# Which pair of gated tiles each place of the down projection takes

## The chip, the cores and the metric

The kernel runs on one core of a Trainium2 chip. The metric is the device time of one execution in microseconds (us); the median of several runs is compared. One profiled execution gives the rows that are quoted. The engines are TensorE (PE, with its weight loads as PEld), VectorE (DVE), ScalarE (ACT), GpSimd (POOL) and SyncE (SP, which here only issues transfers). Each engine works through its own list of instructions in order and waits for the others by semaphores.

## The reference, cut to what matters

The program is one decoder layer over 256 tokens of width 2048 in fp32: a norm, an input projection, attention and pooling heads, an output projection, and then the gated MLP, in which the change lies:

```python
def conv_ffn(h, w_up, conv_w, conv_b, w_down):
    u = h @ w_up                                   # 2048 -> 2 * 5632
    ...                                            # causal convolution of width 3 over the tokens
    gate, val = jnp.split(y, 2, axis=-1)
    return (jax.nn.silu(gate) * val) @ w_down      # 5632 -> 2048
```

The sum over the 5632 gated features may be taken in any order.

## The kernel before

**Splitting.** Each fp32 operand is split into a high part (ACT copies it to `wh`, line 126) and a low part (DVE subtracts, `wl`, line 131), and each product is three matmuls: high by high, low by high and high by low. The weights come in halves of 128 x 1024, one half to a step of the program. The last loop of `layer` runs over these steps: at step u it issues PE's matmuls of step u, the high part of step u+6 and the low part of step u+5, and then what hangs on the step. So the splitting runs five to six steps ahead of PE, on the same ACT and DVE lists that also hold the elementwise work.

**Thirds.** The MLP runs in three thirds of 8, 8 and 6 pairs of gated tiles (a pair is 256 of the 5632 features). For each pair there are two blocks of four steps: the gate block and the value block, each of which accumulates into one PSUM tile of the tag `acc`, which has two buffers. Behind a block, `conv` empties the tile (ACT copies one half, line 451, DVE adds the other, line 452, both written `fs`), multiplies by the norm's factor and runs the convolution. Behind a value block, `value` multiplies by the gate (line 700) and splits the result into `hid` (lines 701 and 702).

**Token sums.** In some places of the down projection a quad (256 features by 1024 outputs by 256 tokens, two by two blocks in each operand) takes seven products of blocks in place of eight, a scheme of Strassen's kind. It needs four sums of blocks of the gated pair. `token_sums` makes them directly behind the pair's `value`: four operations in a row on POOL (line 715), and then the split of the four sums into `sx` by ACT (line 716) and DVE (line 717). ACT's instruction waits for POOL, and the weight splits of the next steps stand behind it on ACT's and DVE's lists.

**Down projection.** When all pairs of a third are made, `down_pair` runs twice, once for each half of the 2048 outputs, over nq places (nq is the number of pairs in the third). Place j takes pair j. `MIXED` says which places go by seven products: 0 and 3 in the first pass and 0, 3, 5 and 6 in the second for eight places; 0, and then 0, 2 and 3, for six. `SUMMED` is their union, {8: [0, 3, 5, 6], 6: [0, 2, 3]}, and before the change it is also the list of pairs for which `token_sums` runs. The first place of a third is one of seven products. Its first half writes into PSUM tiles of other tags, its second half into `ps_down`, two tiles of the tag `acc`: the second of them is the buffer in which the third's last value block was accumulated, and its first matmul (the last of the three groups of three at line 722) must wait until DVE's `fs` (line 452) has emptied it.

Of the kernel before, what the change touches and what calls it, by code (L numbers as in the profile page):

```python
# [57 lines left out]
MIXED = {8: ((0, 3), (0, 3, 5, 6)), 6: ((0,), (0, 2, 3))}  # L58
SECOND = {8: (3, 6), 6: (2,)}
SUMMED = {n: sorted(set(a + b)) for n, (a, b) in MIXED.items()}  # L60


def bucket(n):
# [9 lines left out]
def layer(ctx: ExitStack, tc: tile.TileContext, xT, xtok, wts, par, rel_d, ident_d, icnt_d, out):  # L73
    nc = tc.nc
# [24 lines left out]
    raws, wparts, shift, late = {}, {}, {}, {}  # L99
# [147 lines left out]
    ps = small("ps_start")  # L247
# [253 lines left out]
    steps, hooks = [], []  # L501
# [42 lines left out]
    def after(u, f):  # L544

        hooks.append((u, f))
# [148 lines left out]
    def value(ps, g, j):  # L695
        if j == 0:
            late["hid"] = keep.tile([P, KT, 2, S], F32R, name="hid", tag="c")
        y = conv(ps, NF + 2 * g, 1)
        hid, ks = late["hid"], slice(2 * j, 2 * j + 2)
        nc.vector.tensor_tensor(y, y, late["gate"], op=OP.mult)  # L700
        nc.scalar.activation(hid[:, ks, 0, :], y, AF.Copy)  # L701
        nc.vector.tensor_tensor(hid[:, ks, 1, :], y, hid[:, ks, 0, :].bitcast(F32), op=OP.subtract)
        if j in late["mixed"]:
            token_sums(y, late["mixed"].index(j))

    def token_sums(y, i):

# [16 lines left out]
    def down_pair(bp, nq, final):  # L724


        box, runs, mixed = {}, [], MIXED[nq][bp]
        s_end = 2 * mixed[-1] + 1
        rest = 2 * nq - 1 - s_end

        def hid(k, t):
            return [late["hid"][:, k, a, t * P:(t + 1) * P] for a in range(2)]

        def sums(i, n):
            return [late["sx"][:, i, n, a, :] for a in range(2)]

        def bank(t, b):
            return box["tok"][t][:, b, :]

        def part(w, c):  # L740
            return [p[:, 512 * c:512 * (c + 1)] for p in w]

        def quad_sums(u, j, h):
            if j == 0 and h == 0:
                box["aux"], box["p5"], box["p7"] = aux("ps_p"), small("ps_p5"), small("ps_p7")
                box["tok"] = [acc("ps_down") for t in range(NT)]
            first, last, i = j == 0, j == mixed[-1], SUMMED[nq].index(j)
            if h == 0:
                t13, (s1, s4) = wparts.pop(u + 1), late["s"][seven[u]]
                triple(box["aux"][:, 0, :], hid(2 * j, 0), s1, first, last)  # L750
                triple(box["p5"], sums(i, 0), part(t13, 0), first, last)
                triple(box["p7"], sums(i, 2), part(t13, 1), first, last)
                triple(box["aux"][:, 1, :], sums(i, 1), part(s4, 0), first, last)
            else:
                b2, s4 = wparts.pop(u - 1), late["s"][seven[u - 1]][1]
                triple(bank(0, 1), sums(i, 3), part(b2, 0), first, False, end)
                triple(bank(0, 0), hid(2 * j + 1, 0), part(b2, 1), first, False, end)
                triple(bank(1, 0), hid(2 * j + 1, 1), part(s4, 1), first, False, end)

        def quad(u, j, h):  # L760
            w = wparts.pop(u)
            closes = j == nq - 1 and h == 1
            for n, (a, i) in enumerate(((0, 0), (1, 0), (0, 1))):
                for t in range(NT):
                    for b in range(2):
                        nc.tensor.matmul(bank(t, b), hid(2 * j + h, t)[a], part(w, b if h == 0 else 1 - b)[i],  # L766
                                         start=(t == b == 1 and j == 1 and h == 0 and n == 0), stop=(closes and n == 2),
                                         skip_group_check=end)

        def add_out(t, b, c, src):  # L770
            cols_ = slice((2 * bp + b) * 512 + c.start, (2 * bp + b) * 512 + c.stop)
            x2 = late["x2"][:, t, cols_]
            nc.vector.tensor_tensor(x2, src, x2, op=OP.add)
            return lambda: nc.sync.dma_start(out[:, t, cols_], x2)

        def last_quad(us, j):
            ws = [wparts.pop(u) for u in us]
            full = slice(0, 512)
            add_out(1, 1, full, bank(1, 1))
            ends = [small("ps_end")[:, :256] for _ in range(2)]  # L780
            pieces = [(t, b, full, bank(t, b), False) for t, b in ((0, 0), (0, 1), (1, 0))]
            pieces += [(1, 1, slice(256 * i, 256 * i + 256), ends[i], True) for i in range(2)]
            for t, b, c, ps, first in pieces:
                for h, w in enumerate(ws):
                    w = [p[:, c] for p in part(w, b if h == 0 else 1 - b)]
                    for n, (a, i) in enumerate(((0, 0), (1, 0), (0, 1))):
                        nc.tensor.matmul(ps, hid(2 * j + h, t)[a], w[i], start=(first and h == 0 and n == 0),
                                         stop=(h == 1 and n == 2), skip_group_check=True)
                if t or b:
                    stores = [add_out(t, i, c, bank(t, i)) for i in range(2)] if t == 0 else [add_out(t, b, c, ps)]  # L790
                    for store in stores:
                        store()

        def add_part(n):
            x2 = late["x2"][:, :, 1024 * bp:1024 * (bp + 1)]
            pa_, p7 = box["aux"], box["p7"]
            if n in (0, 2):
                s = late["pool"].tile([P, 4, P], F32, name="s", tag="s").rearrange("p a n -> p (a n)")
                nc.scalar.activation(s, p7 if n else pa_[:, 0, :], AF.Copy)
                nc.vector.tensor_tensor(pa_[:, 1, :], pa_[:, 1, :], s, op=OP.add)  # L800
            elif n == 1:
                nc.vector.tensor_tensor(x2[:, 0, :], pa_.rearrange("p a n -> p (a n)"), x2[:, 0, :], op=OP.add)
            elif n == 3:
                x = x2[:, 1, :].rearrange("p (b n) -> p b n", n=512)
                nc.vector.tensor_tensor(x, pa_[:, 1:2, :].to_broadcast([P, 2, 512]), x, op=OP.add)
            else:
                x = x2[:, :, 512:]
                nc.vector.tensor_tensor(x, box["p5"][:, None, :].to_broadcast([P, 2, 512]), x, op=OP.add)

        def close(u):  # L810
            x2 = late["x2"][:, :, 1024 * bp:1024 * (bp + 1)]
            for t in range(NT):
                nc.vector.tensor_tensor(x2[:, t, :], box["tok"][t].rearrange("p b n -> p (b n)"), x2[:, t, :],
                                        op=OP.add)
                if final:
                    nc.sync.dma_start(out[:, t, 1024 * bp:1024 * (bp + 1)], x2[:, t, :])

        end = final and bp == 1
        for j in range(nq):
            for h in range(2):  # L820
                at = 2 * j + h

                def run(u, j=j, h=h, at=at):
                    if j in mixed:
                        quad_sums(u, j, h)
                    elif end and j == nq - 1:
                        if h == 1:
                            last_quad((u - 1, u), j)
                    else:
                        quad(u, j, h)  # L830
                run.seven = int(bp == 1 and j in SECOND[nq]) if j in mixed and h == 0 else None
                acts = [run]
                for n in range(5):
                    if at == s_end + 1 + n * (rest - 1) // 5:
                        acts.append(lambda n=n: add_part(n))
                if at == 2 * nq - 1 and not end:
                    acts.append(lambda: close(0))
                    run.closes = True
                runs.append(acts)
        return runs  # L840

    for n, (g0, g1) in enumerate(THIRDS):
        after(len(steps), lambda nq=g1 - g0: late.__setitem__("mixed", SUMMED[nq]))
        for g in range(g0, g1):
            steps += feat_block(lambda: late["h"], lambda ps, g=g: gate(ps, g), aux if n and g == g0 else acc)
            steps += feat_block(lambda: late["h"], lambda ps, g=g, j=g - g0: value(ps, g, j))
# [7 lines left out]
    n = len(steps)  # L854
# [29 lines left out]
def chunks(w_in, pool_w, w_out, w_up, w_down):  # L884
# [19 lines left out]
    for g0, g1 in THIRDS:  # L904
        for g in range(g0, g1):
            out += feat(w_up, 256 * g) + feat(w_up, DFF + 256 * g)
        for c0 in range(0, D, 1024):
            for k in range(2 * g0, 2 * g1, 2):
                top, low = (w_down[i * P:(i + 1) * P, c0:c0 + 1024] for i in (k, k + 1))
                out += [top, np.concatenate([low[:, 512:], low[:, :512]], axis=1)]  # L910
    return np.stack([np.concatenate(out[i:i + 2], axis=1) for i in range(0, len(out), 2)])
# [37 lines left out]
```

## Time and profile before

| | |
|---|---|
| median of three runs (lowest, highest) | 1022.37 us (1021.85, 1022.79) |
| profiled execution: its time, its span | 1023.08 us, 1021.3 us |
| mean clock granted to PE | 0.998 |
| PE busy | 1012.7 us, 99% of the span |
| DVE busy | 793.6 us, 78% |
| ACT busy | 554.3 us, 54% |
| POOL busy | 74.7 us, 7% |
| token sums in the program | 11: 44 operations on POOL, 11 on ACT, 11 on DVE |

A row of the trace's list in order of time reads: start in us, duration in us, engine, line, operation, what it writes `<-` what it reads, its shape, how many like it follow one another, and in brackets how long the engine stood idle before it and what ended that. Matmuls overlap: a row's duration is longer than its distance to the next row, so distances between starts are used. The table by stretches gives busy time and, under PEclk, the share of PE's full clock that was granted in the stretch.

### The profile page before, as it was taken

What the parts mean: (1) busy time and instruction counts of PE and PEld (TensorE: products, weight loads), DVE (VectorE), ACT (ScalarE), POOL (GpSimd) and SP (SyncE); (2) the same over time, 40 slices, a digit from 0 to 9 for tenths busy, and PEclk for the clock granted to TensorE, in tenths of its full rate; (3) what the DMA queues carried; (4) which work ended last, traced back from release to release, by engine and by line L of the source; (5) the groups of instructions that cost most, each with busy time, mean ns of one, the idle gap of its engine ahead of it and who ended that gap; (6) DMA issues with size and microseconds to landing.
All of it is one profiled execution on the core that took longest, in us unless ns stands there. A gap on an engine that the chain in (4) does not pass through costs nothing.

```text
span 1021.3 us, 13562 instructions
## 1 busy us (share of the span) xinstructions
PE 1012.7 (99%) x5268; PEld 868.8 (85%) x5268; DVE 793.6 (78%) x994; ACT 554.3 (54%) x747; POOL 74.7 (7%) x98
## 2 busy tenths in 40 slices
PE   9999999999999999999999999999999999999998
PEld 8888888888888888887888888888878888888887
DVE  6966667874567877778998687787899887778897
ACT  6844555564545655555545465565564545556642
POOL 0420004600000000010000000000000000010000
PEclk9999999999999999999999999999999999999999
DMA  9774454475453554444655445455365645545461
GB/s 337 268 286 171 170 175 165 166 296 198 165 197 140 202 210 184 181 165 165 247 207 206 165 168 211 176 199 189 135 243 205 241 164 179 199 166 202 184 233 42
DMA packets 30608, 199.19 MB, mean 195 GB/s; under 512 B 3576, under 2 KB 4472, under 8 KB 7760
## 3 DMA queue, kind: packets, MB, share of 16 engines
q1 hardware_dynamic: 29968, 196.89, 52.6%
q0 software_dynamic: 576, 1.44, 0.6%
q8 instruction: 41, 0.67, 0.3%
q14 instruction: 23, 0.19, 0.1%
HBM read 195.83 MB, written 2.49 MB: 194 GB/s over the span
## 4 chain that ended last, share of the span: by engine, by line
PE 91%; DVE 5%; ACT 2%; issue 1%; POOL 0%; ACTq 0%; DVEq 0%; POOLq 0%
PE ps_feat L187 30%; PE ps_tok L174 17%; PE ps_feat L189 15%; PE ps_down L766 15%; PE ps_v L181 4%; PE ps_p L722 4%; PE ps_down L722 3%; DVE wl L131 2%; ACT wh L126 2%; DVE y L686 1%; PE ps_pool L196 1%; DVE y L684 1%; DVE fs L452 1%; PE ps_s L402 1%; POOL s L715 0%
## 5 line engine op out<-in xcount | busy, mean ns | idle before, releaser
L187 PE MATMUL ps_feat<-x2h,wh 128*128 128x512 f32 x1408 | 488.6, 392 | 0.0
L131 DVE TENSOR_TENSOR wl<-raw,wh 128x1024 fp32r<-128x1024 f32 x358 | 434.8, 1252 | 54.9 <-PE ps_tok L174 27.7
L126 ACT ACTIVATE wh<-raw 128x1024 fp32r<-128x1024 f32 x358 | 360.2, 1050 | 147.2 <-DVE raw L145 69.9
L189 PE MATMUL ps_feat<-x2h,wl 128*128 128x256 f32 x1408 | 393.6, 280 | 0.0
L187 PEld LDWEIGHTS ps_feat<-x2h,wh 128*128 128x128 f32 x1408 | 264.3, 188 | 58.3
L189 PEld LDWEIGHTS ps_feat<-x2h,wl 128*128 128x128 f32 x1408 | 264.3, 188 | 0.1
L766 PE MATMUL ps_down<-wh,hid 128*128 128x512 f32 x432 | 108.3, 393 | 0.0
L766 PEld LDWEIGHTS ps_down<-wh,hid 128*128 128x128 f32 x432 | 82.1, 190 | 17.2
L683 ACT ACTIVATE y<-u,pv 128x256 f32<-128x256 f32 x88 | 48.2, 594 | 74.1 <-DVE u L678 74.1
L174 PE MATMUL ps_tok<-wh,xh 128*128 128x512 f32 x256 | 70.1, 396 | 0.0
L174 PE MATMUL ps_tok<-wh,cat 128*128 128x512 f32 x256 | 68.8, 390 | 0.0
L684 DVE SCALAR_TENSOR_TENSOR y<-u,pv,y 128x256 f32<-128x256 f32 x88 | 42.4, 482 | 29.6 <-ACT y L683 29.6
L715 POOL TENSOR_TENSOR s<-y 128x128 f32<-128x128 f32 x22 | 14.2, 647 | 685.9 <-DVE y L700 429.5
L766 PE MATMUL ps_down<-wl,hid 128*128 128x512 f32 x216 | 57.8, 389 | 0.0
L174 PEld LDWEIGHTS ps_tok<-wh,cat 128*128 128x128 f32 x256 | 47.6, 188 | 9.6
L174 PEld LDWEIGHTS ps_tok<-wh,xh 128*128 128x128 f32 x256 | 47.5, 188 | 9.4
L452 DVE TENSOR_TENSOR fs<-ps_feat,fs 128x512 f32<-128x512 f32 x44 | 30.4, 691 | 29.0 <-ACT fs L451 29.0
L766 PEld LDWEIGHTS ps_down<-wl,hid 128*128 128x128 f32 x216 | 40.7, 188 | 8.5
L187 PE MATMUL ps_feat<-xh,wh 128*128 128x512 f32 x128 | 46.2, 402 | 0.0
L686 DVE SCALAR_TENSOR_TENSOR y<-u,pv,y 128x256 f32<-128x256 f32 x88 | 42.7, 485 | 3.1
L451 ACT ACTIVATE fs<-ps_feat 128x512 f32<-128x512 f32 x44 | 26.1, 592 | 32.7 <-PE ps_feat L189 32.4
L701 ACT ACTIVATE hid<-y 128x512 fp32r<-128x512 f32 x22 | 14.0, 634 | 49.0 <-DVE y L700 49.0
(173 smaller groups left out, 1021.0 us busy)
## 6 DMA issues: line engine op xcount, KB each, us to landing
raw<-in_wts SPq DMA_DIRECT2D x177, 1024.0 KB, 5.0
raw<-in_wts SPq DMA_DIRECT2D x4, 512.0 KB, 7.7
x<-in_xtok SPq DMA_DIRECT2D x1, 2048.0 KB, 9.6
raw<-in_wts SPq DMA_DIRECT2D x7, 256.0 KB, 5.9
xboth<-in_xT SPq DMA_DIRECT2D x4, 256.0 KB, 6.8
T<-band POOLq DMA_DIRECT2D x8, 128.0 KB, 5.7
out<-x SPq DMA_DIRECT2D x2, 512.0 KB, 4.4
out<-x SPq DMA_DIRECT2D x3, 256.0 KB, 2.2
```

Of the source, the lines that this page charges most:

```text
L126: nc.scalar.activation(wparts[u][0], raw(u - 1 if u - 1 in seven else u + 1 if u in seven else u), AF.Copy)
L131: nc.vector.tensor_tensor(wl, raw(u - 1 if u - 1 in seven else u + 1 if u in seven else u), wh.bitcast(F32), op=OP.subtract)
L174: nc.tensor.matmul(ps[:, t, :], act[:, k0 + k, a, t * P:(t + 1) * P], w[:, k * 512:(k + 1) * 512], start=(first and k == 0 and n == 0), st ...
L181: nc.tensor.matmul(ps[:, t, :], act[:, k, a, t * P:(t + 1) * P], w[i], start=(first and n == 0), stop=(last and n == 2))
L187: nc.tensor.matmul(ps, wh[:, ws], act[:, k, :, :], start=(first and n == 0), stop=False, skip_group_check=True)
L189: nc.tensor.matmul(ps[:, S:], wl[:, ws], act[:, k, 0, :], start=False, stop=(last and n == len(ks) - 1), skip_group_check=True)
L452: nc.vector.tensor_tensor(dst, ps[:, :, :S], dst, op=OP.add)
L683: nc.scalar.activation(y[:, m, :], u[:, m, 2:], AF.Identity, scale=cw[2], bias=col(C_CB + f))
L684: nc.vector.scalar_tensor_tensor(y[:, m, :], u[:, m, 1:1 + S], cw[1], y[:, m, :], op0=OP.mult, op1=OP.add)
L686: nc.vector.scalar_tensor_tensor(y[:, m, :], u[:, m, :S], cw[0], y[:, m, :], op0=OP.mult, op1=OP.add)
L722: nc.tensor.matmul(ps, act[a], w[i], start=(first and n == 0), stop=(last and n == 2), skip_group_check=skip)
L766: nc.tensor.matmul(bank(t, b), hid(2 * j + h, t)[a], part(w, b if h == 0 else 1 - b)[i], start=(t == b == 1 and j == 1 and h == 0 and n == ...
```

## The change

Place j now takes pair `ORDER[nq][j]`. The places that go by seven products take the pairs that are made first, and the other places take the rest in rising order:

`ORDER = {8: [0, 4, 5, 1, 6, 2, 3, 7], 6: [0, 3, 1, 2, 4, 5]}`

So `token_sums` runs behind pairs 0, 1, 2, 3 where it ran behind 0, 3, 5, 6 (thirds of eight), and behind 0, 1, 2 where it ran behind 0, 2, 3 (the third of six). The places themselves, with seven or eight products each, stay, and the host lays the rows of `w_down` in the new order, so that the transfers keep their number, size and order.

```diff
+ORDER = {n: [js.index(j) if j in js else len(js) + j - sum(i < j for i in js) for j in range(n)]
+         for n, js in SUMMED.items()}
...
         if j in late["mixed"]:
-            token_sums(y, late["mixed"].index(j))
+            token_sums(y, j)
...
-            first, last, i = j == 0, j == mixed[-1], SUMMED[nq].index(j)
+            first, last, i, k = j == 0, j == mixed[-1], SUMMED[nq].index(j), 2 * ORDER[nq][j]
...
-                triple(box["aux"][:, 0, :], hid(2 * j, 0), s1, first, last)
+                triple(box["aux"][:, 0, :], hid(k, 0), s1, first, last)
...
-                        nc.tensor.matmul(bank(t, b), hid(2 * j + h, t)[a], part(w, b if h == 0 else 1 - b)[i],
+                        nc.tensor.matmul(bank(t, b), hid(2 * ORDER[nq][j] + h, t)[a], part(w, b if h == 0 else 1 - b)[i],
...
-        after(len(steps), lambda nq=g1 - g0: late.__setitem__("mixed", SUMMED[nq]))
+        after(len(steps), lambda nq=g1 - g0: late.__setitem__("mixed", range(len(SUMMED[nq]))))
...
-            for k in range(2 * g0, 2 * g1, 2):
+            for k in (2 * (g0 + g) for g in ORDER[g1 - g0]):
```

PE's and SP's lists and POOL's are the same before and after, by operation, shape, tile name and awaited engine; on ACT and DVE only the split of the sums changes its place. The first place is ACT's list behind the value block of pair 6 of the first third, the last pair but one (rows of `hid` end a pair's `value`; `s512h` is the first weight sum of the down projection, which is split within the steps of the last pair). Before:

```order
L451 ACTIVATE fs<-ps_feat 128x512
L683 ACTIVATE y<-u_1880,pv 128x256 x2
L701 ACTIVATE hid<-y 128x2x256
L716 ACTIVATE sx<-s 128x4x128
L126 ACTIVATE wh<-raw 128x1024 x3
L150 ACTIVATE s512h_1871<-raw 128x512
L126 ACTIVATE wh<-raw 128x1024
```

The same place after the change:

```order
L453 ACTIVATE fs<-ps_feat 128x512
L685 ACTIVATE y<-u_1880,pv 128x256 x2
L703 ACTIVATE hid<-y 128x2x256
L128 ACTIVATE wh<-raw 128x1024 x3
L152 ACTIVATE s512h_1871<-raw 128x512
L128 ACTIVATE wh<-raw 128x1024
```

The row of `sx`, which waits for POOL, is gone from between `hid` and the weight splits (lines are two higher in the changed file). The same holds behind pair 5. The second place is DVE's list behind the value block of pair 1 of the first third. Before:

```order
L700 TENSOR_TENSOR y<-y 128x512
L702 TENSOR_TENSOR hid<-y,hid 128x2x256
L131 TENSOR_TENSOR wl<-raw,wh 128x1024 x4
L452 TENSOR_TENSOR fs<-ps_feat,fs 128x512
L678 TENSOR_TENSOR u_1879<-fs,rrow_2591 128x2x256
```

The same place after the change:

```order
L702 TENSOR_TENSOR y<-y 128x512
L704 TENSOR_TENSOR hid<-y,hid 128x2x256
L719 TENSOR_TENSOR sx<-s,sx 128x4x128
L133 TENSOR_TENSOR wl<-raw,wh 128x1024 x4
L454 TENSOR_TENSOR fs<-ps_feat,fs 128x512
L680 TENSOR_TENSOR u_1879<-fs,rrow_2591 128x2x256
```

The split of the sums now stands behind pair 1, ahead of the four weight splits of the next gate block; ACT's list changes alike there, and both change alike behind pair 2.

More of the change, by code (lines that the diff above doesn't have):

```diff
@@ L756, in quad_sums @@
                 triple(bank(0, 1), sums(i, 3), part(b2, 0), first, False, end)
-                triple(bank(0, 0), hid(2 * j + 1, 0), part(b2, 1), first, False, end)
-                triple(bank(1, 0), hid(2 * j + 1, 1), part(s4, 1), first, False, end)
+                triple(bank(0, 0), hid(k + 1, 0), part(b2, 1), first, False, end)
+                triple(bank(1, 0), hid(k + 1, 1), part(s4, 1), first, False, end)
         def quad(u, j, h):
@@ L786, in last_quad @@
                     for n, (a, i) in enumerate(((0, 0), (1, 0), (0, 1))):
-                        nc.tensor.matmul(ps, hid(2 * j + h, t)[a], w[i], start=(first and h == 0 and n == 0),
+                        nc.tensor.matmul(ps, hid(2 * ORDER[nq][j] + h, t)[a], w[i], start=(first and h == 0 and n == 0),
                                          stop=(h == 1 and n == 2), skip_group_check=True)
```

## The prediction

> **What bounds the kernel now.** The page gives PE 99% of the span, so only a wait of PE can be won. The view of waits for PE has two rows (waited for: us in total, times, longest):
>
> ```profile
> PE ps_down L722 <- DVE fs L452: 4.0, 2, 2.0
> PE ps_start L249 <- DVE ones L246: 1.1, 1, 1.1
> ```
>
> The second is the start. The first is the second half of the first place of a down projection: its last group of matmuls waits for DVE to empty the last value block. There are three thirds but two such waits, so I looked at all three in the order of time: the last matmul before the group, the group, the first matmul of the next place, and, in the first two, the start of the next place of seven products, two ordinary places later.
>
> ```profile
> 475.99 0.39 PE L722 MATMUL ps_down<-wl,hid 128*128 128x512 f32 x1
> 478.38 0.73 PE L722 MATMUL ps_down<-s1024h,hid 128*128 128x512 f32 x2 [2.00 <-DVE fs L452]
> ...
> 479.18 3.57 PE L766 MATMUL ps_down<-wh,hid 128*128 128x512 f32 x8
> ...
> 491.69 0.62 PE L722 MATMUL ps_p<-s512h,hid 128*128 128x512 f32 x2
> ...
> 740.39 0.39 PE L722 MATMUL ps_down<-wl,hid 128*128 128x512 f32 x1
> 742.78 0.73 PE L722 MATMUL ps_down<-s1024h,hid 128*128 128x512 f32 x2 [2.00 <-DVE fs L452]
> ...
> 743.58 1.99 PE L766 MATMUL ps_down<-wh,hid 128*128 128x512 f32 x8
> ...
> 754.47 0.61 PE L722 MATMUL ps_p<-s512h,hid 128*128 128x512 f32 x2
> ...
> 958.80 0.39 PE L722 MATMUL ps_down<-wl,hid 128*128 128x512 f32 x1
> 959.02 0.61 PE L722 MATMUL ps_down<-s1024h,hid 128*128 128x512 f32 x2
> ...
> 959.70 1.98 PE L766 MATMUL ps_down<-wh,hid 128*128 128x512 f32 x8
> ```
>
> The third third passes the same point without a stop: 0.22 us between starts, where the others need 2.39. In the first third the row at 479.18 is also slow (3.57 against 1.99 us for the same eight matmuls). The view by stretches shows why (PE, PEld, DVE, ACT and POOL busy, then PEclk):
>
> ```profile
> 476.00:478.40 2.40, 0.40 (x3) 0.03 (x1) 2.37 (x4) 1.33 (x2) 0.00 (x0) 1.00 1.00 406
> 478.40:480.00 1.60, 1.60 (x5) 1.32 (x6) 0.93 (x2) 0.92 (x2) 0.00 (x0) 0.74 0.98 389
> 480.00:482.00 2.00, 2.00 (x6) 1.59 (x5) 1.89 (x5) 0.17 (x1) 0.00 (x0) 0.50 0.48 197
> 482.00:484.00 2.00, 2.00 (x9) 1.56 (x9) 1.30 (x3) 1.60 (x3) 0.00 (x0) 0.86 0.03 8
> 492.00:500.00 8.00, 8.00 (x37) 6.64 (x36) 7.83 (x8) 6.82 (x8) 0.00 (x0) 1.00 0.89 312
> 744.00:746.00 2.00, 2.00 (x10) 1.64 (x9) 1.81 (x4) 0.58 (x2) 0.00 (x0) 1.00 0.68 279
> ```
>
> Right behind the wait the granted clock falls to half; behind the equal wait of the second third it stays at 1.00.
>
> **Why DVE is late.** ACT and DVE from the end of the last value block but one to the last, first third, then the third third; the first PE row of each is where the down projection begins.
>
> ```profile
> 450.12 0.60 ACT L451 ACTIVATE fs<-ps_feat 128x512 f32<-128x512 f32 x1
> 455.53 0.64 ACT L701 ACTIVATE hid<-y 128x512 fp32r<-128x512 f32 x1 [2.22 <-DVE y L700]
> 457.97 0.64 ACT L716 ACTIVATE sx<-s 128x512 fp32r<-128x512 f32 x1 [1.81 <-POOL s L715]
> 458.51 2.94 ACT L126 ACTIVATE wh<-raw 128x1024 fp32r<-128x1024 f32 x3
> 466.81 0.58 ACT L451 ACTIVATE fs<-ps_feat 128x512 f32<-128x512 f32 x1
> 472.11 0.63 PE L722 MATMUL ps_p<-s512h,hid 128*128 128x512 f32 x2
> 477.64 0.68 DVE L452 TENSOR_TENSOR fs<-ps_feat,fs 128x512 f32<-128x512 f32 x1
> ...
> 932.93 0.60 ACT L451 ACTIVATE fs<-ps_feat 128x512 f32<-128x512 f32 x1
> 938.34 0.64 ACT L701 ACTIVATE hid<-y 128x512 fp32r<-128x512 f32 x1 [2.23 <-DVE y L700]
> 938.88 2.95 ACT L126 ACTIVATE wh<-raw 128x1024 fp32r<-128x1024 f32 x3
> 947.18 0.58 ACT L451 ACTIVATE fs<-ps_feat 128x512 f32<-128x512 f32 x1
> 954.91 0.63 PE L722 MATMUL ps_p<-s512h,hid 128*128 128x512 f32 x2
> 958.01 0.69 DVE L452 TENSOR_TENSOR fs<-ps_feat,fs 128x512 f32<-128x512 f32 x1
> ```
>
> Both begin alike: ACT takes the value block 21.99 and 21.98 us before the down projection. Then the first third has a token sum (pair 6 makes one, pair 4 of the third third doesn't): ACT stands 1.81 us for POOL and copies for 0.64 us, and only then come the weight splits. From `hid` to the next `fs` it takes 466.81 - 455.53 = 11.28 us against 947.18 - 938.34 = 8.84, so 2.44 more. At the end DVE's `fs` starts 477.64 - 472.11 = 5.53 us after the down projection begins, against 958.01 - 954.91 = 3.10: 2.43 more. Nothing on the way has given the sum's delay back, since the pieces of the first weight sums keep both engines in one chain there.
>
> **What the change removes.** Behind pairs 6 and 5 no sum is left, so the first two thirds end as the third one does today. DVE's `fs` then starts at 472.11 + 3.10 = 475.21 and ends 0.69 us later, at 475.90; PE wants it at 475.99 + 0.22 = 476.21. It is ready 0.31 us early, and the wait goes whole. Its price in each third:
> - the gap: 2.39 - 0.22 = 2.17 us, and the group's slower start: 0.80 us to the next row (479.18 - 478.38 and 743.58 - 742.78) against 0.68 (959.70 - 959.02), 0.12 us. Together 2.29 us, twice: 4.58 us.
> - the clock, first third only: the two ordinary places take 491.69 - 479.18 = 12.51 us against 754.47 - 743.58 = 10.89, so 1.62 us.
>
> The sum is 6.20 us. More can't come: PE's list is unchanged and its other wait is not touched. The least is a relief by ACT's copy alone, 458.51 - 457.97 = 0.54 us in each third, if the stop for POOL were covered by something else; I take the whole 2.43, because the third third shows the same list without the sum.
>
> **What it adds.** The sums now stand behind pairs 1 and 2 (pair 1 in the last third), one pair after the other, and ACT's and DVE's weight splits wait behind them. ACT's `fs` rows before and behind pair 5's sum, and two of a stretch without sums, show what that costs:
>
> ```profile
> 350.28 0.60 ACT L451 ACTIVATE fs<-ps_feat 128x512 f32<-128x512 f32 x1 [1.26 <-PE ps_feat L189]
> 361.38 0.60 ACT L451 ACTIVATE fs<-ps_feat 128x512 f32<-128x512 f32 x1 [1.77 <-PE ps_feat L189]
> ...
> 427.94 0.60 ACT L451 ACTIVATE fs<-ps_feat 128x512 f32<-128x512 f32 x1 [1.77 <-PE ps_feat L189]
> ...
> 440.11 0.58 ACT L451 ACTIVATE fs<-ps_feat 128x512 f32<-128x512 f32 x1
> ```
>
> Without sums ACT is at each block's end 1.26 or 1.77 us before PE, and the blocks end 361.38 - 350.28 = 11.10 us apart. Behind the sum the next gate block is taken after 12.17 us, 1.07 late; the value block behind it, at 450.12, 22.18 us after 427.94, which is two blocks, so on the beat again. The idle 1.26 + 1.77 = 3.03 us of a pair hold the 2.44 of a sum, so a sum is repaid within its own pair and a row of them doesn't add up. PE has the five steps of splits in hand: the last gate block of the first third is taken at 466.81, 16.69 us after the block before it instead of 11.10, and no PE row waits for `wh` or `wl`. I put the moved sums at nothing; without that cover each would cost PE the 1.07 us. What the places read is ready: place 1 takes pair 4 (pair 3 in the short third), made pairs earlier, and the last place still takes the last pair.
>
> **The sum.** The profiled execution, 1023.08 us, less 6.20 is 1016.88 us; I predict 1016.9. The median of the runs, 1022.37, lies 0.71 lower. Were its runs without the clock's dip, the change would give 1022.37 - 4.58 = 1017.8; had they the same one, 1022.37 - 6.20 = 1016.2. The likeliest case is 1016.0 to 1018.0. Some 2 us (0.2%) is what can be told from no change.
>
> **Rivals.**
> 1. *The dip has another origin and stays.* Then 1023.08 - 4.58 = 1018.5. For it: one of two equal waits has no dip. Against it: it begins within the 1.6 us behind the wait. Chance 0.08. [...]
> 2. *Part of the wait stays*: only the 0.54 us of the copy passes through, because the transfers or POOL hold the chain. Then 1.75 us of each 2.29 remain, and perhaps the dip: 1023.08 - 1.1 = 1022.0, or 1020.4 without the dip; with half the relief about 1019.5. Against it: the third third, row by row. The margin of 0.31 us is thin, though. Chance 0.05.
> 3. *The gain is given back in the down projection.* DVE is busy 7.83 of 8 us from 492 to 500; if its splits are the bound there, PE runs into them: no change, 1022.4. Against it: DVE moves ahead by 2.43 us and PE by 2.29. Only in the first third does PE gain more than DVE, 3.91 against 2.43, and then it stands to DVE as in the second third, which has no wait. Chance 0.05.
> 4. *Slower: the sums add up.* If a sum's 1.07 us isn't repaid, four in a row leave 4.28 us at pair 3, and the chain at the last pair ends 4.28 - 2.43 = 1.85 us later than now in two thirds, and 3.21 - 0.32 = 2.9 us late in the last: 1022.4 + 3.7 + 2.9 = 1029.0. It decides once a pair's idle time is under the sum's 2.44. Against it: the idle 3.03 us, and the row at 450.12. Chance 0.03.
>
> **How the numbers follow.** The forecast has 0.79. Range 1015.9 to 1019.0: the likeliest case, rival 1, and a part of rival 2. Faster by over 0.2%: the forecast, rival 1 and over half of rival 2, 0.90; no change: rival 3 and the rest of rival 2, 0.06; slower 0.04.
>
> **What would show it.** Right: PE's view of waits keeps only the start's row; in all three thirds the last group of the first place starts 0.22 us after the row before; DVE's `fs` there starts 3.1 us after the down projection begins; the granted clock is 1.00 behind it; behind pairs 1 to 3 the gate block's `fs` is 1.1 us late and the value block's on the beat. Wrong: a wait of PE for `wl`, `wh` or `hid` that is new, a rest of the old wait, or value blocks that are taken later from pair to pair.

## The result, and the profile after

The changed kernel takes 1016.89 us (median of 6 runs, 1016.56 to 1017.67), beside 1022.58 us for the kernel before in the same comparison: a ratio of 0.9945, 95% interval 0.9932 to 0.9957. Its profiled execution takes 1017.18 us with a span of 1015.4 us; that is 5.90 us less than the profiled execution of before.

The view of waits for PE (waited for: us in total, times, longest) has one row left, the start's:

```profile
PE ps_start L251 <- DVE ones L248: 1.1, 1, 1.1
```

PE at the first place of the down projection in the order of time, first and second third: the last matmul before the last group, the group, the first matmul of the next place, and the next place of seven products.

```profile
476.30 0.39 PE L724 MATMUL ps_down<-wl,hid 128*128 128x512 f32 x1
476.52 0.62 PE L724 MATMUL ps_down<-s1024h,hid 128*128 128x512 f32 x2
...
477.20 1.98 PE L768 MATMUL ps_down<-wh,hid 128*128 128x512 f32 x8
...
488.08 0.62 PE L724 MATMUL ps_p<-s512h,hid 128*128 128x512 f32 x2
...
736.78 0.39 PE L724 MATMUL ps_down<-wl,hid 128*128 128x512 f32 x1
737.01 0.62 PE L724 MATMUL ps_down<-s1024h,hid 128*128 128x512 f32 x2
...
737.69 1.98 PE L768 MATMUL ps_down<-wh,hid 128*128 128x512 f32 x8
...
748.57 0.62 PE L724 MATMUL ps_p<-s512h,hid 128*128 128x512 f32 x2
```

The gap is 0.22 and 0.23 us where it was 2.39. From the first row to the last of each third it is now 11.78 and 11.79 us, where it was 15.70 and 14.08: 3.92 and 2.29 us, 6.21 together. The stretches behind the point run at full clock (busy times of the engines, then PEclk):

```profile
476.00:478.00 2.00, 2.00 (x11) 1.65 (x10) 1.30 (x3) 1.04 (x2) 0.00 (x0) 1.00 1.05 365
478.00:480.00 2.00, 2.00 (x11) 1.65 (x10) 1.89 (x5) 0.06 (x1) 0.00 (x0) 1.00 0.50 205
480.00:482.00 2.00, 2.00 (x11) 1.65 (x10) 1.30 (x3) 1.72 (x3) 0.00 (x0) 1.00 0.02 8
```

ACT and DVE from the last value block but one, first third, with the PE row at which the down projection begins:

```profile
450.43 0.60 ACT L453 ACTIVATE fs<-ps_feat 128x512 f32<-128x512 f32 x1 [1.77 <-PE ps_feat L191]
455.84 0.64 ACT L703 ACTIVATE hid<-y 128x512 fp32r<-128x512 f32 x1 [2.23 <-DVE y L702]
464.69 0.58 ACT L453 ACTIVATE fs<-ps_feat 128x512 f32<-128x512 f32 x1
472.42 0.63 PE L724 MATMUL ps_p<-s512h,hid 128*128 128x512 f32 x2
475.51 0.69 DVE L454 TENSOR_TENSOR fs<-ps_feat,fs 128x512 f32<-128x512 f32 x1
```

From `hid` to the next `fs` it is 8.85 us (it was 11.28), and DVE's last `fs` starts 3.09 us after the down projection begins (it was 5.53). It ends at 476.20, 0.32 us before PE takes the tile. The profiled executions differ by 5.90 and not 6.21 because the down projection of the first third begins at 472.42 instead of 472.11. That is not the moved sums: PE waits for nothing between the start and there, and the two executions part in their first 12 us and stay 0.30 us apart from then on. The trace lists a granted clock of 1.00 from 6.04 us on here and from 4.70 us on before, and the first four matmuls that write `ps_v` take 1.53 us here (4.92 to 6.45) and 1.01 before (4.82 to 5.83).

And the sums in a row, ACT behind the value blocks of pairs 1, 2 and 3 of the first third, with the sum behind pair 2:

```profile
361.68 0.60 ACT L453 ACTIVATE fs<-ps_feat 128x512 f32<-128x512 f32 x1
...
369.53 0.64 ACT L718 ACTIVATE sx<-s 128x512 fp32r<-128x512 f32 x1 [1.80 <-POOL s L717]
373.86 0.58 ACT L453 ACTIVATE fs<-ps_feat 128x512 f32<-128x512 f32 x1
383.87 0.60 ACT L453 ACTIVATE fs<-ps_feat 128x512 f32<-128x512 f32 x1
...
406.05 0.60 ACT L453 ACTIVATE fs<-ps_feat 128x512 f32<-128x512 f32 x1
```

The gate block behind the sum is taken after 12.18 us instead of 11.10, and the value blocks are 22.19 and 22.18 us apart: each sum is repaid within its pair.

### The profile page after: what moved, and what is told of

The parts are those of the page before. It is cut to its first block, busy times and chain, and to the rows that moved or that the text cites. A ratio compares the mean times of both kernels' runs of the same rounds, so it can differ in the third digit from the quotient of the medians.

```text
span 1015.4 us, 13562 instructions
## 1 busy us (share of the span) xinstructions
PE 1010.8 (100%) x5268; PEld 868.4 (86%) x5268; DVE 793.4 (78%) x994; ACT 554.7 (55%) x747; POOL 74.7 (7%) x98
## 4 chain that ended last, share of the span: by engine, by line
PE 100%; DVE 0%; issue 0%
PE ps_feat L189 35%; PE ps_feat L191 18%; PE ps_tok L176 17%; PE ps_down L768 14%; PE ps_v L183 4%; PE ps_p L724 4%; PE ps_down L724 3%; PE ps_pool L198 1%; PE ps_s L404 1%; PE ps_start L251 0%; PE ps_down L789 0%; PE ps_x2T L633 0%; PE ps_T L391 0%; PE ps_av L437 0%; PE ps_eT L426 0%; PE ps_av L438 0%
```

## The experiments

All are edits of the changed kernel. Times are medians; the ratio is to the kernel before, with its 95% interval. The mean granted clock is listed for every run, to three places; a dip like the one behind the first wait of before (0.50 for 3.41 us in the profiled execution, from 479.15 us) shows as 0.998.

**One sum put back: pair 5's.**

```diff
-ORDER = {8: [0, 4, 5, 1, 6, 2, 3, 7], ...}   # sums behind pairs 0, 1, 2, 3
+ORDER = {8: [0, 2, 4, 1, 6, 3, 5, 7], ...}   # sums behind pairs 0, 1, 3, 5
```

> The changed kernel with one sum put back: in the thirds of eight, the sums stand behind pairs 0, 1, 3 and 5 (place 5 takes pair 5's predecessor's slot: places 0, 3, 5, 6 take pairs 0, 1, 3, 5). Theory: a sum is repaid within its own pair, so pair 5's does no harm and pair 6's alone made the wait. Then no wait of PE at the first place of a down projection, DVE's last fs 3.1 us after the down projection begins, and 1016.9 us as with the whole change. Rival (both moved sums count, the delay of pair 5 reaches the last pair): a rest of the wait, about half of 2.3 us in two thirds, 1018 to 1020 us.

Measured: 1016.96 us, ratio 0.9944 (0.9931 to 0.9956), and no wait of PE but the start's. DVE's last `fs` and PE's group in the order of time:

```profile
475.27 0.69 DVE L453 TENSOR_TENSOR fs<-ps_feat,fs 128x512 f32<-128x512 f32 x1
...
476.30 0.61 PE L723 MATMUL ps_down<-s1024h,hid 128*128 128x512 f32 x2
```

It is the time of the whole change. Pair 5's sum did no harm, and moving it brought nothing.

**The other one put back: pair 6's.**

```diff
-ORDER = {8: [0, 4, 5, 1, 6, 2, 3, 7], ...}
+ORDER = {8: [0, 3, 4, 1, 5, 2, 6, 7], ...}   # sums behind pairs 0, 1, 2, 6
```

> The opposite half: sums behind pairs 0, 1, 2 and 6 in the thirds of eight, so pair 5's is moved and pair 6's stays. Theory: both waits are back whole, a gap of 2.39 us between starts at the last group of the first place in the first two thirds, DVE's last fs 5.5 us after the down projection begins, and the kernel's time is that of the kernel before, 1022.4 us, with the clock's dip behind the gaps in some executions (1021.5 without one). Rival (the order in which PE reads the pairs, or the number of sums near the end, counts): a time between 1017 and 1020 us.

Measured: 1022.16 us, ratio 0.9996 (0.9987 to 1.0005). Same place, first third:

```profile
477.21 0.68 DVE L453 TENSOR_TENSOR fs<-ps_feat,fs 128x512 f32<-128x512 f32 x1
...
477.94 0.91 PE L723 MATMUL ps_down<-s1024h,hid 128*128 128x512 f32 x2 [1.99 <-DVE fs L453]
```

The view of waits for PE has the second third's wait too:

```profile
PE ps_down L723 <- DVE fs L453: 4.0, 2, 2.0
```

The kernel before is back, waits and time. In the thirds of eight the single sum behind the last pair but one is the whole cause.

**The sum behind the very last pair.** Place 6 takes pair 7, place 7 pair 6.

```diff
-ORDER = {8: [0, 4, 5, 1, 6, 2, 3, 7], ...}
+ORDER = {8: [0, 3, 4, 1, 5, 2, 7, 6], ...}   # sums behind pairs 0, 1, 2, 7
```

> Sums behind pairs 0, 1, 2 and 7 in the thirds of eight: place 6 takes pair 7 and place 7 takes pair 6. The sum of the very last pair stands behind DVE's last fs on the lists, so it can't hold up that fs; it holds up the weight splits of the down projection by 2.4 us instead. Theory: no wait at the first place, and the splits have five steps in hand, so 1016.9 us. Rival (DVE's splits bound the down projection, rival 3 of the prediction): PE waits for wl or wh within the down projection, up to 2.4 us in two thirds, 1019 to 1022 us.

Measured: 1020.83 us, ratio 0.9982 (0.9973 to 0.9990). The wait at the first place is gone, as the theory has it, but the rival's loss is there, in two thirds, by the view of waits for PE:

```profile
PE ps_p L723 <- DVE wl L132: 1.4, 2, 0.7
PE ps_p L723 <- ACT wh L127: 1.0, 2, 0.5
```

PE and DVE at place 3 of the first pass:

```profile
488.06 0.39 PE L723 MATMUL ps_p<-s512l,hid 128*128 128x512 f32 x1
488.92 0.73 PE L723 MATMUL ps_p<-wh,sx 128*128 128x512 f32 x2 [0.48 <-ACT wh L127]
490.34 0.50 PE L723 MATMUL ps_p<-wl,sx 128*128 128x512 f32 x1 [0.69 <-DVE wl L132]
...
489.07 1.22 DVE L132 TENSOR_TENSOR wl<-raw,wh 128x1024 fp32r<-128x1024 f32 x1
```

The same low part and the same matmul in the changed kernel:

```profile
487.14 1.22 DVE L133 TENSOR_TENSOR wl<-raw,wh 128x1024 fp32r<-128x1024 f32 x1
...
488.54 0.39 PE L724 MATMUL ps_p<-s512l,hid 128*128 128x512 f32 x1
...
489.21 0.39 PE L724 MATMUL ps_p<-wl,sx 128*128 128x512 f32 x1
```

There it ends at 488.36, 0.85 us before PE wants it. The five steps in hand are a margin of 0.85 us at place 3: the places of seven products need DVE's differences of the weights (1.23, 0.69 and 0.69 us) on top of the splits. A sum's 2.4 us there costs 1.6 us in each of two thirds (490.34 - 488.06 = 2.28 us against 489.21 - 488.54 = 0.67), and 1.7 with the slower matmuls right behind the two stops. That is 3.5 of the 3.6 us by which the two profiled executions differ from the begin of the first down projection (471.94 and 472.42) to the end; the medians differ by 3.94 us.

**The wait made in the third that had none.**

```diff
-ORDER = {..., 6: [0, 3, 1, 2, 4, 5]}   # sums behind pairs 0, 1, 2
+ORDER = {..., 6: [0, 2, 1, 4, 3, 5]}   # sums behind pairs 0, 1, 4
```

> The changed kernel, but in the last third (six pairs) the sums stand behind pairs 0, 1 and 4, so that its last pair but one makes a sum as pair 6 did in the others before. Theory: the wait appears in the third where it never was: DVE's last fs 2.43 us later, 5.5 us after the down projection begins, a gap of 2.39 us, and 1016.9 + 2.3 = 1019.2 us, or 1020.8 with the clock's dip behind it. Rival (the third third is spared for another reason, its shorter length or its place in the program): no gap, 1016.9 us.

Measured: 1021.36 us, ratio 0.9982 (0.9973 to 0.9991). DVE's last `fs` and PE's group in the last third:

```profile
954.42 0.69 DVE L453 TENSOR_TENSOR fs<-ps_feat,fs 128x512 f32<-128x512 f32 x1
...
955.17 0.73 PE L723 MATMUL ps_down<-s1024h,hid 128*128 128x512 f32 x2 [2.00 <-DVE fs L453]
```

The wait is there, with the 2.00 us that the first two thirds had before. The runs fall into two groups: four at 1018.97 to 1019.43 us with a mean clock of 0.999 or 1.000, and seven at 1021.10 to 1021.68 us with 0.998. The first is the expected 2.3 us over the changed kernel; the second, with the dip, is 2.2 us longer.

**The stop for POOL made longer.** On the kernel with pair 6's sum, POOL's last operation behind pair 6 is done three or five times; the second run differs in the number alone.

```diff
+            for _ in range(1 + (more if n == 3 else 0)):      # more = 2, then 4, behind pair 6
-            nc.gpsimd.tensor_tensor(s[:, n, :], a, b, op=op)
+                nc.gpsimd.tensor_tensor(s[:, n, :], a, b, op=op)
```

> The kernel with sums behind pairs 0, 1, 2 and 6, and behind pair 6 the last of POOL's four operations is done three times instead of once (same values). It lengthens the stop of ACT for POOL by two operations of about 0.5 us. Theory (the gap is that one chain): the gap at the first place grows one for one, from 2.39 to about 3.4 us in two thirds, and the time by 2.0 us over that of the kernel with the single operation, 1024.5 us; if the clock falls behind a long enough gap, it now falls in more executions, by 1.6 us each. Rival (something else than the sum sets DVE's end): gap and time stay, 1022.5 us.

> As the one before, with POOL's last operation behind pair 6 done five times. Theory: gap about 4.4 us in two thirds, 4 us over the kernel with the single operation, 1026.5 us, and with a gap this long the clock falls behind both gaps in nearly every execution, some 1.6 us each, so up to 1028 us. If the dip had nothing to do with the gap: no more dips than with the single operation, 1026 us at most.

Measured: 1025.91 us, ratio 1.0031 (1.0020 to 1.0042), and 1027.89 us, ratio 1.0053 (1.0038 to 1.0068). PE at the first place of the first third, with two operations more:

```profile
471.80 0.63 PE L724 MATMUL ps_p<-s512h,hid 128*128 128x512 f32 x2
...
473.39 0.50 PE L724 MATMUL ps_p<-wl,sx 128*128 128x512 f32 x1 [0.26 <-DVE wl L132]
...
479.13 1.22 PE L724 MATMUL ps_down<-s1024h,hid 128*128 128x512 f32 x2 [2.13 <-DVE fs L453]
```

With four more:

```profile
472.65 0.63 PE L724 MATMUL ps_p<-s512h,hid 128*128 128x512 f32 x2
...
475.32 0.49 PE L724 MATMUL ps_p<-wl,sx 128*128 128x512 f32 x1 [1.34 <-DVE wl L132]
...
481.06 1.22 PE L724 MATMUL ps_down<-s1024h,hid 128*128 128x512 f32 x2 [2.13 <-DVE fs L453]
```

From the down projection's begin to the group it takes 7.33 and 8.41 us, and 6.26 with the single operation: 1.07 and 1.08 us per two operations, one for one with POOL's 0.54 each. I had expected the gap to grow; it stays at 2.1 us, and the rest turns up earlier, at the low weights of the first place, which the same chain makes. The dip shows in six of seven runs and in four of four; with the single operation it was four of eleven. A dip behind both gaps, as expected for the longest stop, didn't come: its four runs have 0.998, which is one dip each, and only two of the seven runs with two operations more have 0.997.

**Every sum twice.**

```diff
-            token_sums(y, j)
+            for _ in range(2):
+                token_sums(y, j)
```

> The changed kernel with every token sum made twice over (same values), behind pairs 0 to 3, and 0 to 2 in the last third. A second sum adds about four operations of POOL at 0.55 us, ACT's 0.64 and DVE's 0.69, 3.5 us, to the first one's 2.4, together 5.9 us of delay per pair against 3.0 us of idle time. Theory (a sum is free as long as the pair's idle time holds it, and adds up beyond): value blocks are taken about 2.9 us later from pair to pair, 11 us at pair 3, PE waits there or at the down projections, and the time is 5 to 12 us over the changed kernel, 1022 to 1029 us. Rival (five steps of splits in hand hold any sums that stand early in a third): 1016.9 us.

Measured: 1045.91 us, ratio 1.0233 (1.0216 to 1.0250), more than expected. The first row of the view of waits for PE, and ACT at the value blocks of pairs 0 to 3:

```profile
PE ps_feat L191 <- DVE wl L133: 18.6, 8, 2.9
```

```profile
316.95 0.60 ACT L453 ACTIVATE fs<-ps_feat 128x512 f32<-128x512 f32 x1 [1.77 <-PE ps_feat L191]
...
342.29 0.58 ACT L453 ACTIVATE fs<-ps_feat 128x512 f32<-128x512 f32 x1
...
367.68 0.57 ACT L453 ACTIVATE fs<-ps_feat 128x512 f32<-128x512 f32 x1
...
393.07 0.57 ACT L453 ACTIVATE fs<-ps_feat 128x512 f32<-128x512 f32 x1
```

The blocks are 25.3 to 25.4 us apart in place of 22.2: 3.2 us per pair, where 2.9 was expected. Beyond the idle time sums do add up. What I had wrong is how much of that the five steps absorb: PE waits for low weights in every pair with doubled sums but the first of each third, eight times and 18.6 us, and the mean clock falls to 0.993 with these waits (0.91 from 340 to 360 us, where PE is busy for 17.17 of the 20 us), which alone is some 7 us by estimate (0.007 of 1044 us). The two make up most of the 29.0 us over the changed kernel.

**More places of seven products.** Since the changed PE is bound by its matmuls alone, fewer matmuls were tried.

```diff
-MIXED = {8: ((0, 3), (0, 3, 5, 6)), 6: ((0,), (0, 2, 3))}
+MIXED = {8: ((0, 3, 5), (0, 3, 5, 6)), 6: ((0, 2), (0, 2, 3))}
```

> The changed kernel with one more place of seven products in the first pass of each third (places 0, 3 and 5 of eight, 0 and 2 of six; the sums that they need are made already). PE saves 3 of 24 matmuls at 0.227 us in three places, 2.04 us. Theory: the down projection's splits have room, so 1014.9 us. Rival (DVE and ACT, at 98% in the down projection's first places, can't hold the extra weight sums, about 2.6 us of DVE and 1 us more for each): PE waits for splits and the gain is lost, 1017 to 1020 us.

Measured: 1044.9 us, ratio 1.0219 (1.0204 to 1.0234). As edited, the weight sums of the added place go into the one set of buffers before the last place's are read, so the place before it is multiplied by the wrong sums, and reading and writing take turns. The first two rows of the view of waits for PE:

```profile
PE ps_p L724 <- ACT s512h L152: 8.9, 3, 3.6
PE ps_down L724 <- ACT s1024h L152: 3.9, 1, 3.9
```

Its time says nothing of the seven products, so the mended form was run, with both sets of buffers in turn and in the thirds of eight only:

```diff
-MIXED = {8: ((0, 3), (0, 3, 5, 6)), 6: ((0,), (0, 2, 3))}
+MIXED = {8: ((0, 3, 5), (0, 3, 5, 6)), 6: ((0,), (0, 2, 3))}
...
-                run.seven = int(bp == 1 and j in SECOND[nq]) if j in mixed and h == 0 else None
+                run.seven = int((bp == 1 or nq == 8) and j in SECOND[nq]) if j in mixed and h == 0 else None
```

> The changed kernel with place 5 of the first pass of the two thirds of eight taken by seven products too, and with the two sets of buffers of the weight sums used in turn in that pass as in the second one (place 3 takes the second set), so that the sums of the next place are not written while the last ones are still to be read. PE saves 3 matmuls of 0.227 us in two thirds, 1.36 us. In the changed kernel the low part for place 3 ends 0.85 us before PE wants it. Theory now: that margin is all the room the splits have in the first pass, and place 5 adds about 2.6 us of DVE and 0.6 us of ACT before it, so PE waits at place 5 for weight sums or splits, 1 to 3 us in each of two thirds, and the time is 1017 to 1022 us. Rival (places 3 to 5 let the splits catch up): no wait, 1015.5 us.

Measured: 1022.13 us, ratio 1.0000 (0.9991 to 1.0010). The view of waits for PE without the start:

```profile
PE ps_p L724 <- DVE x L807: 2.6, 2, 1.3
PE ps_p L724 <- DVE x L810: 1.3, 2, 0.6
PE ps_down L724 <- DVE x L815: 1.1, 2, 0.6
```

The time is in the range, but for another reason: nothing waits at place 5. The wait is at the begin of the second pass, for the adds (lines 807, 810 and 815) that empty the first pass's products. They start only behind the last place of seven products, which is now two places later. From the last group of the first pass to the first ordinary place of the second it takes 8.95 us in the first third (512.35 to 521.30) against 5.66 in the changed kernel (513.70 to 519.36), 3.29 us more; twice that, less the 1.36 saved, is 5.2 us, the whole loss against the changed kernel. A version that empties these products sooner was not run. No version tried beats the changed kernel.

## Why the prediction was right, point by point

- *What bounds the kernel.* PE's one wait that could be won was where the view of waits put it. Both of its waits went, and nothing took their place.
- *Why DVE is late.* 2.44 us from `hid` to the next `fs` and 2.43 at the end were predicted; 2.43 (11.28 - 8.85) and 2.44 (5.53 - 3.09) were measured. The third third was a true model of the other two; with the sum put behind its own last pair but one, it waits like them.
- *The terms.* Gap and slower start 2.29 us twice, clock 1.62 us: 6.20 predicted, 6.21 in the rows. The margin was given as 0.31 us and is 0.32.
- *The moved sums at nothing.* Right in the rows: 1.08 us late at the gate block, on the beat at the value block. The condition, an idle time over a sum's cost, held up in the doubled sums. The cover is smaller than I had it, though: "PE has the five steps of splits in hand" was read from one late block, and in the doubled sums PE waits from the second pair on.
- *Time.* 1016.9 predicted, 1016.89 measured; the medians of the comparison differ by 5.69 us. It rests in part on luck: the 6.20 us were read from an execution with a dip and taken from that execution's time, and the dip is there in some executions and not in others. Of the 50 runs of the kernel before in the comparisons of the experiments, 30 have a mean clock of 1.000 and a median of 1021.91 us, and 20 have 0.998 or less and 1023.0 us. Against the 20 the change saves 6.1 us, near the 6.20; against the 30 it saves 1021.91 - 1016.89 = 5.0 us, 0.4 more than the 4.58 of the gaps alone. What that rest is stays open, as no execution of the kernel before without a dip was profiled. The start is a candidate: it moves the begin of the first down projection by up to 0.97 us between the profiled executions (471.68 to 472.65).
- *Rival 1, the dip has another origin.* Fell. In 22 runs without such a gap (the changed kernel, pair 5's sum put back, the last pair's sum) the mean clock is 1.000 in every one. Why only one of two equal waits has a dip behind it is not shown by any run.
- *Rival 2, part of the wait stays.* Fell, with the margin of 0.32 us. Half the relief would have been 1023.08 - 2.29 - 1.62 = 1019.2 us, not 1019.5; and by the rivals' own chances no change has 0.07 and slower 0.03, where 0.06 and 0.04 are given.
- *Rival 3, the gain is given back in the down projection.* It didn't come, but the argument against it, that the second third runs at that distance without a wait, hid how near it is: 0.85 us at place 3. The sum behind the last pair shows it at work.
- *Rival 4, the sums add up.* Fell for single sums; the doubled ones show its mechanism, at 3.2 us per pair.

## What to carry to other kernels

Here an instruction that waited for a third engine held up what stood behind it on its own list (ACT's `sx` stood 1.81 us for POOL, and ACT's next `fs` came 2.44 us later), and what that cost depended on where it stood: the same sum was free behind a pair that has 3.0 us of idle time to repay it, and cost 2.3 us and sometimes the clock just before a point where PE needs the buffer back. Where a program repeats a stage with small differences, compare the repetition that does not wait with those that do, row by row; the difference names the cause, its size and the margin. And move such work to where it is repaid before the next deadline, not simply away: behind the last pair the same sum missed the deadline after it.

## What the runs showed of the hardware that was not expected

- Behind a stop of PE of 2.39 us between starts, 2.00 us of it idle, the granted clock fell to half in some executions and not in others. In the profiled execution of before PE starts again at 478.38 us, and the clock is 0.50 from 479.15 us on, for 3.41 us. By the mean clock (0.998 or less) it fell with one such stop in seven of eleven runs, with two in 20 of 50 runs of the kernel before and in four of eleven with pair 6's sum. In 11 runs with stops of 0.86 and 1.19 us (the last pair's sum: 488.06 to 488.92 and the row at 490.34) the mean clock is 1.000 throughout.
- Of stops of much the same length some have a dip and some have none. In the profiled executions of before and of pair 6's sum PE is idle for 2.0 us in each of the first two thirds, and the clock falls to 0.50 in the first alone (480:482 and 479:481); in the second it stays at 1.00. With the stop for POOL longer, 2.1 us idle in each, it falls in both thirds with two operations more (479:481 and 746:748) and in the first alone with four (481:483). With the wait in the last third, 2.00 us idle, it stays at 1.00 from 954 to 962 us. What decides between them is not shown.
- What a dip costs is much the same in the traces. From the last group of the first place to the next place of seven products the first third takes 13.31 us in the profiled execution of before (478.38 to 491.69), 13.29 with pair 6's sum (477.94 to 491.23), and 13.20 and 13.24 with the longer stops (479.13 to 492.33 and 481.06 to 494.30), each with a dip, against 11.69 in the second third of before (742.78 to 754.47), which has none: 1.5 to 1.6 us. By estimate the 3.41 us at half clock in the trace of before can't cost more than 1.7. The groups of runs with and without a dip lie 1.1 us apart for the kernel before and 2.2 us for the one with the wait in its last third, so they differ in something else too. Whether that is the start isn't shown.
